# First norm of a two-layer encoder trunk: squares and means moved to other engines, inputs fetched in another order, and large tiles placed at multiples of 512 bytes

## The chip, the cores and the metric

The kernel runs on one core of one Trainium2 chip. The metric is the device time of one execution in microseconds (us); lower is better. A core has a tensor engine (TensorE, PE in the profile, with its weight loads as PEld), a vector engine (VectorE, DVE), a scalar engine (ScalarE, ACT), GpSimd (POOL) and a sync engine (SyncE, SP), which issues most of the transfers between the chip's memory and the on-chip SBUF. Each engine works through its own list of instructions in order and waits for the others by semaphores.

## What is computed

Two layers of a streaming encoder, on 512 tokens of 1,024 channels in float32. The change is in the first normalisation of the first layer; the rest of the program uses its result.

```python
def rms_norm(x, g):
    xf = x.astype(jnp.float32)
    y = xf * lax.rsqrt(jnp.mean(xf * xf, axis=-1, keepdims=True) + EPS_RMS)
    return (y * g.astype(jnp.float32)).astype(x.dtype)
...
    c_act = jax.nn.silu(c)
    for l in range(DEPTH):
        mod = c_act @ ada_w[l] + ada_b[l]
        sh1, sc1, gt1, sh2, sc2, gt2 = [m[:, None, :] for m in jnp.split(mod, 6, axis=-1)]
        h = rms_norm(x, norm1_g[l]) * (1 + sc1) + sh1
        p = h @ w_in[0]
        ...
        x = x + gt1 * (mixed @ w_out[l])
        h2 = rms_norm(x, norm2_g[l]) * (1 + sc2) + sh2
        gate, up = jnp.split(h2 @ w_gu[l], 2, axis=-1)
        x = x + gt2 * ((jax.nn.silu(gate) * up) @ w_down[l])
    return rms_norm(x, final_g)
```

## The kernel before, in words

**Layout.** Activations lie with channels on the 128 partitions and the 512 tokens along the row: x is eight tiles of 128 x 512, one for each block k of 128 channels (`xin`, named `xi` in the profile). A weight matrix comes in tiles of 128 x 1,024, eight blocks of 128 x 128.

**Products.** Nearly every product is made from three passes with float32r operands: weights and activations are each split into a high part (a rounded copy made by ScalarE) and a low part (the difference, made by VectorE or by an accumulating transfer that POOL issues), and `block` (L227) multiplies high by high, high by low and low by high. `hh` and `hl` are the parts of the normed activations, `whi` and `wlo` those of the weights, `f` (also `fh10` and such) those of the hidden layer in the feed-forward part. The feed-forward part uses 256-column passes (a seven-product scheme, `seven`), the rest mostly 512-column ones. A product of plain float32 operands (`nh` by `wr`, or the sums of the norm) takes two passes.

**Memory.** SBUF is filled by pools in the order in which they are opened: `const` (constants, L132), then `wraw`, `whl` (the split weights, L134), `hp` (`hh` and `hl`, L135) from the left, others such as `third`, `fp` (feed-forward weights and hidden parts) and `sm` from the right. No size is rounded up, so that each pool begins where the one before ends: in the built program the large tiles of `hp`, `whl` and `wraw` begin 96 bytes past a multiple of 512, those of `fp`, `dn`, `ya` and `third` 480 bytes past one, those of `w0`, `mx`, `wo` and `wk` 160 bytes past one.

**The head** (`head`, L294) comes before the two layers. SyncE issues, in this order: c copied to all 128 partitions (`cact`, 512 KB), the eight tiles of x (256 KB each), the first constants (`cst`) and the columns of biases (`cols`), two rows of `ada` (512 KB each), the first 384 columns of six tiles of `w_in` (`wr`), four more rows of `ada`, the other columns of `w_in`, and so on. ScalarE puts c through Silu (L310), then squares x tile by tile (`square`, L398 and L401), and VectorE adds the squares into one tile, `ssum` (L402). `rstd` (L404) then has TensorE sum `ssum` over the partitions against a column of 1/1024 (L410), ScalarE take the root (L413), VectorE the reciprocal (L414) and four 128 x 128 diagonals of it (`dg`, L417), and TensorE spread the result over all partitions by a product with ones (L422).

**After the norm** each channel block k needs `modulation` (L258: one row of `ada` times c, summed along the row; VectorE, an instruction of line 264), once for the scale and once for the shift, then VectorE's product of x and the norm (`nt`, L354), ScalarE's scale and shift (`nh`, L356), and the split into `hh` and `hl`. For k below `WHOLE` = 3 TensorE multiplies `nh` itself, in float32, by six tiles of `w_in`; from k = 3 on it uses the split parts.

**The order** of instructions on each engine is fixed when the program is built, by a scheduler that follows the code's order where `pinned` (for TensorE) or `exact` (for the other engines) is set.

Of the kernel before, what the change touches and what calls it, by code (L numbers as in the profile page):

```python
# [12 lines left out]
F32 = mybir.dt.float32  # L13
F32R = mybir.dt.float32r
AF = mybir.ActivationFunctionType
ALU = mybir.AluOpType
PSUM = bass.MemoryType.PSUM
DRAM = bass.MemoryType.DRAM

P = 128  # L20
D = 1024
S = 512
L = 2
KC = D // P
# [50 lines left out]

WHOLE = 3

EARLY = ((2, 5, 5, 4), (3, 6, 6, 6))
# [15 lines left out]
ALL = slice(0, S)  # L94
# [27 lines left out]
class Trunk:  # L122
    def __init__(self, ctx, tc, a, out):
# [6 lines left out]
        nc = self.nc  # L130
# [14 lines left out]
        self.omm = [self.const.tile([P, 15], F32, name=f"omm{l}") for l in range(L)]  # L145
        self.omka = [self.const.tile([P, 4], F32, name=f"omka{l}") for l in range(L)]
        self.xs = [self.dram.tile([P, S], F32, name=f"xs{k}") for k in range(KC)]
        self.yb = {
# [5 lines left out]
    def pool(self, **k):  # L154
        if "space" in k:
            return self.tc.tile_pool(**k)
        return self.tc.tile_pool(reuse_waits="tile", **k)
# [136 lines left out]
    def head(self, w0):  # L294
# [3 lines left out]
        self.cact = self.const.tile([P, D], F32, name="cact")  # L298
        nc.sync.dma_start(self.cact, a["c"].partition_broadcast(P))
        xin = [w0.tile([P, S], F32, name=f"xi{k}", bufs=1) for k in range(KC)]  # L300
        for k in range(KC):
            nc.sync.dma_start(xin[k], a["x"][k])
        at = CST["block"][0]
        nc.sync.dma_start(self.cst[:, 0:at], a["cst"][:, 0:at])
        nc.sync.dma_start(self.cols, a["cols"])
        nc.gpsimd.memset(self.ones, 1.0)
        nc.gpsimd.memset(self.mean, 1.0 / D)
        nc.gpsimd.memset(self.eps[:, 0:1], EPS_RMS)
        nc.gpsimd.memset(self.eps[:, 1:2], EPS_GN)
        nc.scalar.activation(self.cact, self.cact, AF.Silu)  # L310
        raws, ws = {}, []

        def rows(k):
            for i in (KC + k, k):
                raws[i] = self.rows(0, i, w0)

        raw = [w0.tile([P, D], F32, name=f"wr{i}", bufs=1) for i in range(KRV0)]
        cut = WHOLE * P
        rows(0)
        for i in range(KRV0):  # L320
# [4 lines left out]
        for i in range(KRV0):  # L325
            at = 0 if i == GV else cut
            nc.sync.dma_start(raw[i][:, at:], a["w_in"][0, i][:, at:])
        for k in range(KC):
            self.square(xin[k], k, ALL)
        self.soon(AF.Sqrt)  # L330
        self.new_h()
        rb = self.rstd(ALL)
        self.soon(AF.Sigmoid)
# [14 lines left out]
        for k in range(KC):  # L348
            if k >= WHOLE:
                rows(k)  # L350
            self.modulation(0, (KC + k, k), raws)
            self.gains(0, 0, k, k + 1)
# [50 lines left out]

    def rstd(self, hs, between=lambda: None):  # L404

        nc = self.nc
        n = (hs.stop - hs.start) // P
        st = self.m()
        for w in range(n):
            at = hs.start + w * P  # L410
            self.mm(st[:, w : w + 1], self.ssum[:, at : at + P], self.mean, start=True, stop=True)
        r = self.tmp.tile([P, 4], F32, tag="r4", name="r4", bufs=2)
        nc.scalar.activation(r[:, 0:n], st[:, 0:n], AF.Sqrt, bias=self.eps[:, 0:1])  # L413
        nc.vector.reciprocal(r[:, 0:n], r[:, 0:n])  # L414
        dg = self.tmp.tile([P, S], F32, tag="sq", name="dg", bufs=2)
        for w in range(n):
            nc.vector.tensor_scalar(  # L417
                dg[:, w * P : (w + 1) * P], self.c("ident"), r[:, w : w + 1], None, ALU.mult
            )
        between()  # L420
        rb = st[:, 0 : n * P]
        self.mm(rb, self.ones, dg[:, 0 : n * P], start=True, stop=True)  # L422
        return rb

    def turned(self, hs, g):
# [3 lines left out]
        st = self.m()  # L429
        r = self.tmp.tile([P, 4], F32, tag="r4", name="r4", bufs=2)  # L430
        out = self.hb[1].tile([P, n, D], F32, tag="hf1", name="y", bufs=1)
# [1235 lines left out]
```

## Time and profile before

| what | value |
|---|---|
| three runs | 1474.26, 1478.91 and 1479.97 us (median 1478.91) |
| profiled execution, its own time | 1479.65 us |
| span of its instructions | 1477.9 us |
| TensorE busy | 1429.7 us, 97% of the span |
| VectorE busy | 1087.3 us, 74% |
| ScalarE busy | 751.0 us, 51% |
| GpSimd busy | 246.8 us, 17% |
| mean rate of the transfers | 203 GB/s |

The profiled execution is one execution; its span runs from the first to the last instruction, and its own time is 1.75 us longer. A busy TensorE means that some pass was in it, not that it ran at its best pace: passes overlap, so the distance between the starts of two passes says more than the duration of one. "The granted clock" is the share of full speed (2.4 GHz) that TensorE was given. A row of the timeline gives the start in us, the duration in us, engine, line, operation, output<-inputs, shape and count, and in brackets how long the engine had been idle before it and what it waited for.

### The profile page before, as it was taken

The page shows a single profiled execution, that of the slowest core. Times are in us where ns is not written, and L with a number is a line of the kernel's source. Part 1 is how long each engine was busy: PE and PEld are TensorE (multiplying, and loading weights), DVE is VectorE, ACT ScalarE, POOL GpSimd, SP SyncE. Part 2 cuts the span into 40 slices and gives each one's busy share as a digit, 9 for nine tenths or more (in the row PEclk, how much of TensorE's full clock was granted, in tenths as well). Part 3 has the DMA queues.
Part 4 walks back from the last instruction along what each step waited for, and adds up shares of the span by engine and source line. Part 5 has one row for each costly group of instructions (what it writes and reads, how often), then busy time and mean ns, then how long its engine had stood idle before and what let it go on. Part 6 is the DMA issues. An engine that isn't in the chain of part 4 may idle for free. (4 is left out here: it accounts for less than half of the span.)

```text
span 1477.9 us, 25375 instructions
## 1 busy us (share of the span) xinstructions
PE 1429.7 (97%) x9982; PEld 1219.6 (83%) x9982; DVE 1087.3 (74%) x1846; ACT 751.0 (51%) x1031; POOL 246.8 (17%) x291
## 2 busy tenths in 40 slices
PE   5999998999999999999999999999999999999998
PEld 2767676777899999988897777877789999998887
DVE  7888958576788888876767685768578888887333
ACT  5576544344456656642336766443444656656221
POOL 0133321110022211100012334111102222110000
PEclk9999999999999999999999999999999999999999
DMA  8788689589839999778726747976974899885232
GB/s 319 235 268 238 193 227 254 148 261 271 236 101 230 234 215 226 179 251 287 260 87 180 181 113 168 261 176 191 289 235 131 208 219 223 192 187 169 87 100 71
DMA packets 112918, 299.28 MB, mean 203 GB/s; under 512 B 12128, under 2 KB 22624, under 8 KB 112800
## 3 DMA queue, kind: packets, MB, share of 16 engines
q1 hardware_dynamic: 90160, 227.93, 47.3%
q0 software_dynamic: 21776, 68.69, 25.5%
q8 instruction: 78, 1.28, 0.4%
q10 hardware_dynamic: 864, 1.05, 0.2%
q14 instruction: 40, 0.33, 0.1%
HBM read 269.84 MB, written 27.79 MB: 201 GB/s over the span
## 5 line engine op out<-in xcount | busy, mean ns | idle before, releaser
L221 PE MATMUL acc<-hh,whi 128*128 128x512 f32 (+1 forms) x1119 | 392.5, 357 | 0.2
L221 PE MATMUL acc<-hh,wlo 128*128 128x512 f32 (+1 forms) x1111 | 379.2, 346 | 8.3 <-DMA wlo<-in_w_in 7.5
L221 PE MATMUL acc<-hl,whi 128*128 128x512 f32 (+2 forms) x1119 | 369.3, 346 | 0.1
L195 ACT CAST whi<-raw 128x1024 fp32r<-128x1024 f32 x143 | 149.8, 1049 | 266.8 <-PE acc L221 175.2
L221 PEld LDWEIGHTS acc<-hh,wlo 128*128 128x128 f32 x1111 | 210.7, 190 | 36.7 <-DMA wlo<-in_w_in 9.2
L221 PEld LDWEIGHTS acc<-hh,whi 128*128 128x128 f32 x1119 | 212.1, 190 | 31.9 <-issue 2.4
L221 PEld LDWEIGHTS acc<-hl,whi 128*128 128x128 f32 (+1 forms) x1119 | 203.8, 189 | 26.4 <-issue 2.2
L201 DVE TENSOR_TENSOR wlo<-raw,whi 128x1024 fp32r<-128x1024 f32 x78 | 94.7, 1221 | 77.3 <-ACT whi L195 72.9
L221 PE MATMUL acc<-f,whi 128*128 128x512 f32 (+1 forms) x304 | 92.2, 386 | 0.0
L221 PE MATMUL m<-tl,f13h 128*128 128x256 f32 x304 | 86.0, 283 | 0.0
L221 PE MATMUL m<-th,f13l 128*128 128x256 f32 x304 | 86.0, 283 | 0.0
L221 PE MATMUL m<-th,f13h 128*128 128x256 f32 x304 | 85.9, 283 | 0.0
L241 ACT CAST f24h<-x 128x1024 fp32r<-128x1024 f32 x38 | 39.9, 1050 | 60.4 <-DVE x L241 60.4
L198 ACT ACTIVATE wlo<-raw 128x1024 fp32r<-128x1024 f32 x65 | 68.5, 1053 | 0.1
L221 PEld LDWEIGHTS acc<-f,whi 128*128 128x128 f32 x304 | 56.2, 188 | 12.3
L199 POOL DMA_DIRECT2D wlo<-in_w_in x41 | 35.9, 876 | 159.3 <-ACT wlo L198 159.3
L1283 POOL DMA_DIRECT2D f22l<-in_w_gu x38 | 32.8, 863 | 171.6 <-ACT f22l L241 164.4
L221 PE MATMUL acc<-f,wlo 128*128 128x512 f32 (+1 forms) x152 | 58.7, 386 | 0.0
L241 DVE TENSOR_TENSOR f24l<-x,f24h 128x1024 fp32r<-128x1024 f32 x38 | 46.5, 1224 | 16.3 <-ACT f24h L241 16.3
L221 PEld LDWEIGHTS m<-th,f13h 128*128 128x128 f32 x304 | 58.4, 192 | 0.0
L221 PEld LDWEIGHTS m<-th,f13l 128*128 128x128 f32 x304 | 58.4, 192 | 0.0
L221 PEld LDWEIGHTS m<-tl,f13h 128*128 128x128 f32 x304 | 58.2, 192 | 0.0
(338 smaller groups left out, 3434.0 us busy)
## 6 DMA issues: line engine op xcount, KB each, us to landing
raw<-in_w_in SPq DMA_DIRECT2D x63, 512.0 KB, 4.7
raw<-in_w_gu SPq DMA_DIRECT2D x50, 512.0 KB, 4.5
raw<-in_w_down SPq DMA_DIRECT2D x44, 512.0 KB, 3.5
wlo<-in_w_in POOLq DMA_DIRECT2D x41, 512.0 KB, 7.7
wlo<-in_w_gu POOLq DMA_DIRECT2D x40, 512.0 KB, 6.8
x<-in_w_gu SPq DMA_DIRECT2D x76, 256.0 KB, 4.4
row<-in_ada SPq DMA_DIRECT2D x30, 512.0 KB, 5.2
raw<-in_ada SPq DMA_DIRECT2D x25, 512.0 KB, 4.9
```

The lines of the kernel that those rows point to most:

```text
L195: self.on(nc.scalar, "copy")(hi, raw)
L198: nc.scalar.activation(lo, raw, AF.Copy, scale=-1.0)
L199: nc.gpsimd.dma_start(lo, src, accum_op=ALU.add)
L201: self.on(nc.vector, "tensor_tensor")(lo, raw, hi.bitcast(F32), ALU.subtract)
L221: i = (tensor.transpose if transpose else tensor.matmul)(*args, **k).ins
L241: return (lambda *a, **k: self.tc.keep_in_program_order(op(*a, **k))) if self.exact else op
L1283: nc.gpsimd.dma_start(lo, two[:, b], accum_op=ALU.add)
```

## The change

Four things change in the head, and one in the placing of tiles.

1. **Order of the transfers.** x goes ahead of c; c is fetched once, into one partition (4 KB), and TensorE spreads it over the partitions by a product with ones, in two halves (`spread`), from which ScalarE makes Silu. `cst`, `cols` and the first row of `ada` move in among the tiles of x.
2. **Squares.** VectorE squares six tiles of x, ScalarE two (k = 3 and 5). Nothing is added on VectorE; TensorE sums each square over the partitions as it comes and accumulates the eight in PSUM (32 products of one column, in place of 4).
3. **TensorE kept at work.** 16 products of ones by ones of 128 columns stand at its start, and five more on either side of the product that spreads the norm. Their results are not used.
4. **Order.** `modulation` for the first scale and the first shift is put ahead of and behind the norm's chain; two of the four diagonals go to ScalarE.
5. **Places.** A pad of 88 floats in `const` and one of 120 floats at the right edge move all pools: in the built program the tiles of `hp`, `whl`, `wraw`, `third`, `fp`, `dn`, `ya`, `w0`, `mx`, `wo` and `wk` begin at multiples of 512 bytes. Of the 7,538 float32r products 68 (in `sm` and `sl`) are left whose operands don't.

```diff
+PADS = (88, 120)
+WARM = (16, 5)
+ORDER = (0, 1, 2, 4, 3, 6, 5, 7)
...
+        self.const.tile([P, PADS[0]], F32, name="pad")
+        pool(name="edge", bufs=1, side="right").tile([P, PADS[1]], F32, name="edge")
...
-        nc.sync.dma_start(self.cact, a["c"].partition_broadcast(P))
         xin = [w0.tile([P, S], F32, name=f"xi{k}", bufs=1) for k in range(KC)]
+        c = w0.tile([1, D], F32, name="c", bufs=1)
+        raws, ws = {}, []
+
+        def rows(k, which=(KC, 0)):
+            for i in which:
+                raws[i + k] = self.rows(0, i + k, w0)
+
+        at = CST["block"][0]
         for k in range(KC):
             nc.sync.dma_start(xin[k], a["x"][k])
-        at = CST["block"][0]
-        nc.sync.dma_start(self.cst[:, 0:at], a["cst"][:, 0:at])
-        nc.sync.dma_start(self.cols, a["cols"])
+            if k == 1:
+                nc.sync.dma_start(c, a["c"].rearrange("(p n) -> p n", p=1))
+            if k == 3:
+                nc.sync.dma_start(self.cst[:, 0:at], a["cst"][:, 0:at])
+                nc.sync.dma_start(self.cols, a["cols"])
+            if k == 5:
+                rows(0, (KC,))
+        rows(0, (0,))
...
-        nc.scalar.activation(self.cact, self.cact, AF.Silu)
-        raws, ws = {}, []
-
-        def rows(k):
-            for i in (KC + k, k):
-                raws[i] = self.rows(0, i, w0)
+        self.soon(AF.Silu)
+        self.pinned = True
+        ps = [self.m() for _ in range(3)]
+        idle = lambda n: [self.mm(ps[2][:, 0:P], self.ones, self.ones, start=True, stop=True) for _ in range(n)]
+        idle(WARM[0])
+
+        def spread(i):
+            cs = slice(i * S, i * S + S)
+            self.mm(ps[i], self.ones[0:1, :], c[:, cs], start=True, stop=True)
+            nc.scalar.activation(self.cact[:, cs], ps[i], AF.Silu)
...
-        rows(0)
...
-        for k in range(KC):
-            self.square(xin[k], k, ALL)
-        self.soon(AF.Sqrt)
+        st = self.m()
+        for n, k in enumerate(ORDER):
+            if n in (1, 2):
+                spread(n - 1)
+                if n == 2:
+                    self.soon(AF.Sqrt)
+            sq = w0.tile([P, S], F32, tag="sq", name="sq", bufs=4)
+            if k in (3, 5):
+                nc.scalar.activation(sq, xin[k], AF.Square)
+            else:
+                nc.vector.tensor_tensor(sq, xin[k], xin[k], ALU.mult)
+            for w in range(4):
+                self.mm(
+                    st[:, w : w + 1], sq[:, w * P : w * P + P], self.mean, start=n == w == 0, stop=n == KC - 1 and w == 3
+                )
+        self.exact = True
+        self.modulation(0, (KC,), raws)
         self.new_h()
-        rb = self.rstd(ALL)
+        rb = self.rstd(ALL, lambda: idle(WARM[1]), st)
+        idle(WARM[1])
+        self.modulation(0, (0,), raws)
+        self.exact = self.pinned = False
...
-            self.modulation(0, (KC + k, k), raws)
+            if k:
+                self.modulation(0, (KC + k, k), raws)
...
-        for w in range(n):
-            nc.vector.tensor_scalar(
-                dg[:, w * P : (w + 1) * P], self.c("ident"), r[:, w : w + 1], None, ALU.mult
-            )
+        for w in range(n):
+            o = dg[:, w * P : (w + 1) * P]
+            if n == 4 and w % 2:
+                self.on(nc.scalar, "activation")(o, self.c("ident"), AF.Copy, scale=r[:, w : w + 1])
+            else:
+                self.on(nc.vector, "tensor_scalar")(o, self.c("ident"), r[:, w : w + 1], None, ALU.mult)
```

In the built programs the order of every engine is the same from the first `nh` on. Three places differ. TensorE, from its first instruction to the first product with `w_in` (`m` and `acc` are PSUM tiles, `mean` the column of 1/1024), before:

```order
L1656 UNCONDITIONAL_BRANCH
L221 MATMUL m<-mean,ssum 128x1 x4
L221 MATMUL m<-dg,ones 128x512
L221 MATMUL acc<-nh,wr_147 128x512
L221 MATMUL acc<-nh,wr_148 128x512
```

TensorE at the same place, changed:

```order
L1700 UNCONDITIONAL_BRANCH
L229 MATMUL m<-ones 128x128 x16
L229 MATMUL m<-mean,sq 128x1 x4
L229 MATMUL m<-c,ones 128x512
L229 MATMUL m<-mean,sq 128x1 x4
L229 MATMUL m<-c,ones 128x512
L229 MATMUL m<-mean,sq 128x1 x24
L229 MATMUL m<-ones 128x128 x5
L229 MATMUL m<-dg,ones 128x512
L229 MATMUL m<-ones 128x128 x5
L229 MATMUL acc<-nh,wr_177 128x512
L229 MATMUL acc<-nh,wr_178 128x512
```

Ahead of the norm's spreading there now stand 55 products in place of 4. ScalarE from its start to the norm's root (`r`), before:

```order
L310 ACT_TABLE_LOAD
L310 ACTIVATE cact<-cact 128x1024
L398 ACTIVATE ssum<-xi_124 128x512
L401 ACTIVATE sq<-xi_125 128x512
L401 ACTIVATE sq<-xi_126 128x512
L401 ACTIVATE sq<-xi_127 128x512
L401 ACTIVATE sq<-xi_128 128x512
L401 ACTIVATE sq<-xi_129 128x512
L401 ACTIVATE sq<-xi_130 128x512
L401 ACTIVATE sq<-xi_131 128x512
L391 ACT_TABLE_LOAD
L391 ACTIVATE soon<-eps 128x2
```

ScalarE at the same place, changed (`soon` is an activation that only calls for a function's table):

```order
L432 ACT_TABLE_LOAD
L432 ACTIVATE soon<-eps 128x2
L339 ACTIVATE cact<-m 128x512 x2
L432 ACT_TABLE_LOAD
L432 ACTIVATE soon<-eps 128x2
L359 ACTIVATE sq<-xi_131 128x512
L359 ACTIVATE sq<-xi_133 128x512
L455 ACTIVATE r_277<-m,eps 128x4
L249 ACTIVATE dg<-cst,r_277 128x128 x2
```

Two squares are left, and they stand behind both halves of Silu and the load of the root's table. SyncE's queue up to the first tile of `w_in`, changed (before: c, the eight tiles of x, `cst`, `cols`, two rows of `ada`):

```order
L317 DMA xi_128<-in_x 128x512
L317 DMA xi_129<-in_x 128x512
L319 DMA c<-in_c 1x1024
L317 DMA xi_130<-in_x 128x512
L317 DMA xi_131<-in_x 128x512
L321 DMA cst<-in_cst 128x128
L322 DMA cols<-in_cols 128x238
L317 DMA xi_132<-in_x 128x512
L317 DMA xi_133<-in_x 128x512
L263 DMA raw<-in_ada 128x1024
L317 DMA xi_134<-in_x 128x512
L317 DMA xi_135<-in_x 128x512
```

c no longer stands ahead of x; `cst`, `cols` and one row of `ada` now stand ahead of its last tile.

## Rows read from the trace of the kernel before

**Rows 1.** The page's first part: busy time, share of the span and instructions

```profile
PE 1429.7 (97%) x9982; PEld 1219.6 (83%) x9982; DVE 1087.3 (74%) x1846; ACT 751.0 (51%) x1031; POOL 246.8 (17%) x291
```

**Rows 2.** The timeline of the head, 0 to 28 us

```profile
0.74 0.21 POOL L306 MEMSET ones<- 128x128 f32 x1 [0.29 <-POOLq L1661]
...
5.43 1.06 ACT L310 ACTIVATE cact<-cact 128x1024 f32<-128x1024 f32 x1 [3.40 <-DMA cact<-in_c]
...
7.55 5.47 DVE L402 TENSOR_TENSOR ssum<-ssum,sq 128x512 f32<-128x512 f32 x7 [7.55 <-ACT sq L401]
...
12.12 1.28 ACT L391 ACT_TABLE_LOAD   x1
...
13.17 1.84 PE L221 MATMUL m<-mean,ssum 128*128 128x1 f32 x8 [13.17 <-POOL omka L383]
...
15.05 0.27 ACT L413 ACTIVATE r<-m,eps 128x4 f32<-128x4 f32 x1 [1.43 <-PE m L221]
...
15.56 0.88 DVE L417 TENSOR_SCALAR dg<-cst,r 128x128 f32<-128x128 f32 x4
16.35 1.28 DVE L264 CUSTOM_DVE_ANT_0 raw<-raw,cact,cols 128x1024 f32<-128x1024 f32 x1
...
16.58 2.04 PE L221 MATMUL m<-dg,ones 128*128 128x512 f32 x2 [1.57 <-DVE dg L417]
...
18.66 1.28 DVE L354 TENSOR_TENSOR nt<-xi,m 128x512 f32<-128x512 f32 x2 [1.03 <-PE m L221]
...
20.25 4.60 PE L221 MATMUL acc<-nh,wr 128*128 128x512 f32 x6 [1.63 <-ACT nh L356]
...
24.69 2.74 PE L221 MATMUL m<-nh,wr 128*128 128x512 f32 x6
```

**Rows 3.** The tiles of x (view of one tile): their issues, and issue to landing

```profile
L302 SPq DMA_DIRECT2D xi<-in_x x8: 328/432/652, 1.2 to 5.4; - x8
...
DMA to landing us min/median/max: 4.8/5.4/6.0
```

**Rows 4.** Busy time by stretch: length, PE, PEld, DVE, ACT, POOL, granted clock, DMA share, GB/s

```profile
10.00:20.00 10.00, 3.88 (x10) 2.28 (x10) 7.50 (x16) 5.62 (x9) 1.65 (x4) 1.00 1.05 396
...
20.00:38.74 18.74, 18.49 (x42) 8.37 (x43) 17.72 (x31) 9.30 (x15) 0.15 (x2) 1.00 0.77 298
...
160.37:167.19 6.82, 4.54 (x8) 2.29 (x9) 6.75 (x9) 2.13 (x3) 3.06 (x3) 0.50 0.18 71
```

**Rows 5.** The timeline where channel block k = 3 comes to TensorE

```profile
37.20 0.82 ACT L356 ACTIVATE nh<-nt,mods,gsc 128x512 f32<-128x512 f32 x1 [4.44 <-DVE mods L264]
...
38.74 1.10 PE L221 MATMUL acc<-hh,whi 128*128 128x512 f32 x4
```

**Rows 6.** The timeline at a later norm: weight loads of the one-column sums

```profile
398.22 0.52 PEld L221 LDWEIGHTS m<-mean,ssum 128*128 128x128 f32 x4 [1.41 <-DVE ssum L402]
```

**Rows 7.** The timeline of TensorE in the last w_down: 512-column passes, hh, then f

```profile
1419.64 0.39 PE L221 MATMUL acc<-hl,whi 128*128 128x512 f32 x1
...
1421.22 0.39 PE L221 MATMUL acc<-hh,wlo 128*128 128x512 f32 x1
...
1421.91 0.40 PE L221 MATMUL acc<-f,wlo 128*128 128x512 f32 x1
...
1423.31 0.40 PE L221 MATMUL acc<-f,wlo 128*128 128x512 f32 x1
```

**Rows 8.** The chain that ended last, in order of time: 256-column passes (start, us, what)

```profile
1176.25 2.88 PE m L221 x24
...
1182.01 1.42 PE m L221 x12
```

**Rows 9.** The timeline of TensorE: 256-column passes with weights from wk

```profile
413.79 0.63 PE L221 MATMUL acc<-hl,whi 128*128 128x256 f32 x4
...
415.20 0.64 PE L221 MATMUL acc<-hl,whi 128*128 128x256 f32 x4
```

**Rows 10.** Who waited for whom: us in total, times, longest

```profile
PE acc L221 <- DMA wlo<-in_w_in: 7.5, 4, 3.1
```

More of the change, by code (lines that the diff above doesn't have):

```diff
@@ L402, in square, with rstd @@
             nc.vector.tensor_tensor(self.ssum[:, hs], self.ssum[:, hs], sq[:, hs], ALU.add)
-    def rstd(self, hs, between=lambda: None):
+    def rstd(self, hs, between=lambda: None, st=None):
         nc = self.nc
         n = (hs.stop - hs.start) // P
-        st = self.m()
-        for w in range(n):
-            at = hs.start + w * P
-            self.mm(st[:, w : w + 1], self.ssum[:, at : at + P], self.mean, start=True, stop=True)
-        r = self.tmp.tile([P, 4], F32, tag="r4", name="r4", bufs=2)
+        if st is None:
+            st = self.m()
+            for w in range(n):
+                at = hs.start + w * P
+                self.mm(st[:, w : w + 1], self.ssum[:, at : at + P], self.mean, start=True, stop=True)
+        r = self.const.tile([P, 4], F32, tag="r4", name="r4", bufs=2)
         nc.scalar.activation(r[:, 0:n], st[:, 0:n], AF.Sqrt, bias=self.eps[:, 0:1])
-        nc.vector.reciprocal(r[:, 0:n], r[:, 0:n])
+        self.on(nc.vector, "reciprocal")(r[:, 0:n], r[:, 0:n])
         dg = self.tmp.tile([P, S], F32, tag="sq", name="dg", bufs=2)
         for w in range(n):
-            nc.vector.tensor_scalar(
-                dg[:, w * P : (w + 1) * P], self.c("ident"), r[:, w : w + 1], None, ALU.mult
-            )
+            o = dg[:, w * P : (w + 1) * P]
[3 more added lines that the diff above has]
+                self.on(nc.vector, "tensor_scalar")(o, self.c("ident"), r[:, w : w + 1], None, ALU.mult)
         between()
@@ L429, in turned @@
         st = self.m()
-        r = self.tmp.tile([P, 4], F32, tag="r4", name="r4", bufs=2)
+        r = self.const.tile([P, 4], F32, tag="r4", name="r4", bufs=2)
         out = self.hb[1].tile([P, n, D], F32, tag="hf1", name="y", bufs=1)
```

## The prediction

> **What bounds the kernel now.** I read the page's busy times first: TensorE is busy for 97% of the span [rows 1], so a change pays only where it takes time from TensorE's list or from what TensorE waits for. Next the timeline of the head [rows 2]: TensorE's first pass starts at 13.17 and its first product with a weight at 20.25, so the head is the longest stretch in which it has nothing to do. The chain there is plain to follow: squares and their sum end on VectorE at 13.02 (7.55 + 5.47), the eight passes of the means take 1.84, ScalarE's root starts at 15.05, the diagonals on VectorE at 15.56, their product with ones runs from 16.58 to 18.62, and VectorE's first `nt` starts at 18.66. TensorE is at half pace here: six passes with `nh` take 4.60 at 20.25 and the next six take 2.74.
>
> Then I looked at what holds TensorE after its start, since a shorter head is worth only what the next bound lets through. Between 20 and 38.74 VectorE is busy for 17.72 of 18.74 us [rows 4], and at k = 3 the supply is just in time: `nh` waits 4.44 us for VectorE, starts at 37.20, its rounded copy follows, and TensorE's first pass with it is at 38.74 [rows 5]. So from there on the clock that counts is VectorE's, counted from `nt` at 18.66; what TensorE gains between 20.25 and 38.74 by itself it would lose again waiting at k = 3. As no engine's order changes behind the first `nh`, the worth of all edits to the head is how much earlier that first `nt` starts.
>
> Last, the pace of the passes themselves, for the new places of the tiles. In the last part of `w_down` passes of one form and one weight pool stand side by side: with `hh` as the moving operand (96 past a multiple of 512, as the weights are) starts lie (1421.22 - 1419.64) / 7 = 0.226 apart, with `f` (480 past one) (1423.31 - 1421.91) / 6 = 0.233 [rows 7]. The only difference that I see between them is where the operands start.
>
> **The head, step by step.** *Transfers.* Before, the last tile of x is issued at 5.4 and lands 5.4 later, at about 10.8 [rows 3]. The change takes 512 KB (c) from ahead of it and puts 64 + 119 + 512 KB (`cst`, `cols`, a row of `ada`) there: 183 KB more, 0.5 us at 396 GB/s [rows 4]. I put it at 11.3. *Squares.* VectorE's square of a 128 x 512 tile costs about what an `nt` costs, 0.64 [rows 2], less than the spacing of the tiles; so they could be done at 12.0, against 13.02.
>
> *TensorE.* It is here that the time goes. The 16 idle products are 32 passes. A pass of this kind at half pace costs 1.84 / 8 = 0.23, and at full pace four weight loads take 0.52 together, the last one's tail included [rows 2, 6]; I take 0.11. In the trace it took from 20.25 to about 24.7 to come to full pace, and I let it need some 4 us from 1.0, when `ones` is set (0.74 + 0.21) [rows 2]. That is 17 passes at half pace and 15 at full, and the idle work ends near 6.6. Then the sums: 64 passes x 0.11 = 7.0, and the two products that spread c, four passes of 512 columns at 2.74 / 6 = 0.46, are 1.8. ScalarE's two squares stand behind the second half of Silu (0.6, half of 1.06 with its fixed part) and a table load of 1.28 [rows 2], and the fifth tile in TensorE's order needs the first of them: I count 1.0 of waiting. Sum: 6.6 + 7.0 + 1.8 + 1.0 = 16.4 for the root, against 15.05. TensorE, not the arrival of x, sets the end of the norm.
>
> *From the root to `nt`.* Before 3.61 (15.05 to 18.66). With two of four diagonals on ScalarE VectorE saves 2 x 0.22; the product with ones at full pace saves 1.0 of 2.04. But the row of `ada` (1.28 and the reading of its sum, some 1.36, as at 16.35 [rows 2]) still stands between the diagonals and `nt` on VectorE: 0.51 + 0.44 + 1.36 = 2.3. `nt` starts at 18.7, as before. The head's worth is **0.0**, between these bounds: -3.3 if the root follows the last tile at once (12.0 + 8 x 0.11 + 0.1 = 13.0, so `nt` at 15.4), and +11 if TensorE stays at half pace (first rival). The two products of five idle passes fit into waits of TensorE (1.1 us each) and cost nothing while it runs at full pace; 512 KB fewer to fetch is 0.2% of the traffic, and nothing waits for it.
>
> **The places of the tiles.** The built program has 684 passes with `f` against weights at 96, 634 with `hh` against weights at 480 or 160, and 1,608 with both at the same offset. If only the offset between the operands counts, all become equal, and 512-column passes go at 0.226: 684 x 0.007 = 4.8 saved in `w_down`, where nothing but TensorE sets the pace; and at the same price 4.4 for the 634. Of these last I count half, 2.2, since TensorE also waits there for others (7.5 us for low parts of `w_in` alone [rows 10]). For 256-column passes the sign turns round: 24 with equal offsets take 2.88, 0.120 each, 12 of the 1,088 at 96 against 480 take 1.42, 0.118 [rows 8], and 12 of the 384 at 96 against 160 take 1.41, 0.1175 [rows 9]. That gives back 1,088 x 0.0017 + 384 x 0.0025 = 2.8. Sum: -4.8 - 2.2 + 2.8 = -4.2; counting all of the 634 it is -6.4. I take **-4**. No row shows a tile at 0, and so both ends stay open: -16, if all passes run at the best pace seen (4,304 of 256 columns at 0.1175 instead of 0.119 on average: 7; and 9 for the others), and +11, if 0 is like the slow pairs (1,608 x 0.007).
>
> A rule speaks against this term. The Trainium skill says that TensorE reads its moving operand and its weights through two ports of their own, so that loading the next weights takes nothing from the pass that runs (TensorE: Matmul & The Clock Gate, Step-by-step: what each phase is for); by it the term would be 0. The trace doesn't agree: 0.226 and 0.233 for the same form of pass [rows 7].
>
> **Sum.** 1479.65 (the profiled execution's own time) + 0.0 - 4 = 1475.65. The median of the runs shown lies 0.74 below that execution; so I predict **1475.0**. A measurement of this kernel can tell 0.5%, 7.4 us, from no change.
>
> **The rivals.** (1) *Slower: the one-column sums don't bring TensorE to full pace, or let it fall back.* The idle work then ends at 1.0 + 32 x 0.23 = 8.4, the sums take 64 x 0.22 = 14.1, c's spreading 3.6: the root is at 26, 11 us later than before, and VectorE's stream with it: 1479.65 + 11 - 4 = 1486.7. It decides against the change once the root comes 4 us late, at 19. For it: such passes ran at half pace at 13.17 [rows 2], and at 160.37 the granted clock was 0.50 after a wait, with 4.54 of 6.82 us busy [rows 4]. Against it: idle products of 128 columns stand ahead of them. The Trainium skill says that half rate is the default and activity lifts it (TensorE: Matmul & The Clock Gate, Part 1: The HAM clock gate); what one-column passes count for isn't said there.
>
> (2) *The head gains in full*: sums that keep up with the arrival of x give -3.3, and the places in full -6.4: 1470.0. For it: 64 passes at 0.11 take no longer than the tiles need to arrive (4.8 to 6.0 after issues at 1.2 to 5.4 [rows 3]); against it: the idle products and c's spreading stand in the same list.
>
> (3) *The places give more*, all passes at the best pace seen: 1479.65 - 16 = 1463.7.
>
> (4) *The change doesn't do what it says*: neither the head nor the places move anything, as the skill's rule on the ports has it: 1479.6. For it: VectorE's bound at k = 3.
>
> **How the numbers follow.** Forecast 0.47, rival (1) 0.10, (2) 0.18, (3) 0.08, (4) 0.17. The range of 1464 to 1486 takes in the forecast, (2), (4), most of (3) and the low part of (1), where half pace holds for a part of the sums only. Faster by over 0.5% are (2) and (3) and a little of the forecast: 0.29. Slower are (1) and a tail of unfavourable places: 0.11. Within 0.5%: 0.60. The likeliest case alone spans 1471 to 1479.
>
> **What would show it.** Right: the root near 16.4 and `nt` near 18.7; TensorE without a gap from 1.0 on, its sums 0.11 apart; a new wait of about 2 us at k = 3; passes of `f` in `w_down` 0.226 apart and those of 256 columns all at 0.120. Wrong: a root before 14 or after 19; passes of `f` still at 0.233, or 512-column passes well below 0.226; VectorE's stream from `nt` to k = 3 shorter than the 18.5 us of before; a granted clock of 0.50 in other stretches than before.

## The result and the profile after

The changed kernel takes 1485.34 us (median of 14 runs, 1481.97 to 1493.17) against 1478.32 for the kernel before, measured on the same chip beside it: a ratio of 1.0061, 95% interval 1.0046 to 1.0076. The ratio leaves out one run of the kernel before that took 4585.17 us, and the quotient of the two medians is 1.0047. The forecast was 1475.0, a little faster; the change is slower by 0.6%. The profiled execution took 1482.6, with a span of 1480.5.

The page's first part says that TensorE is busier than before [rows 1], by 18.6 us and 112 passes, which are 56 products of two passes each (26 idle ones, 28 more sums and two that spread c):

```profile
PE 1448.3 (98%) x10094; PEld 1244.0 (84%) x10094; DVE 1084.9 (73%) x1843; ACT 747.6 (51%) x1029; POOL 245.6 (17%) x291
```

The timeline of the head of the changed kernel (start, length, engine, line, what; in brackets the idle time before it and what ended that) stands against [rows 2]:

```profile
1.00 6.79 PE L229 MATMUL m<-ones 128*128 128x128 f32 x32 [1.00 <-POOL mean L327]
...
7.62 0.95 PE L229 MATMUL m<-mean,sq 128*128 128x1 f32 x8
...
8.50 1.12 PE L229 MATMUL m<-c,ones 1*128 1x512 f32 x2
...
9.55 1.05 PE L229 MATMUL m<-mean,sq 128*128 128x1 f32 x8
...
10.54 2.02 PE L229 MATMUL m<-c,ones 1*128 1x512 f32 x2
11.50 0.69 DVE L361 TENSOR_TENSOR sq<-xi 128x512 f32<-128x512 f32 x1 [2.50 <-DMA xi<-in_x]
...
12.49 10.40 PE L229 MATMUL m<-mean,sq 128*128 128x1 f32 x48
...
16.10 0.69 DVE L361 TENSOR_TENSOR sq<-xi 128x512 f32<-128x512 f32 x1 [3.91 <-PE m L229]
...
22.93 0.26 ACT L455 ACTIVATE r<-m,eps 128x4 f32<-128x4 f32 x1 [7.18 <-PE m L229]
...
25.02 1.91 PE L229 MATMUL m<-dg,ones 128*128 128x512 f32 x2
...
26.98 1.28 DVE L395 TENSOR_TENSOR nt<-xi,m 128x512 f32<-128x512 f32 x2 [1.85 <-PE m L229]
```

Read it by TensorE. Eight one-column passes take 0.95 at 7.62 and eight 1.05 at 9.55; then two passes that spread c take 2.02 where two took 1.12 before, and 48 one-column passes take 10.40, 0.217 each. ScalarE's root starts at 22.93 instead of 15.05, and the first `nt` at 26.98 instead of 18.66: 8.3 us later. The squares are not what is late. The last one waits 3.91 us for TensorE (for a buffer that the sums had not yet read), and ScalarE waits 7.18 for the sums.

The same stretches in the view of busy time by stretch (length, then PE, PEld, DVE, ACT and POOL busy, granted clock, DMA share, GB/s) show what halved the pace. The edges are those at which the granted clock changes:

```profile
1.00:7.21 6.21, 6.21 (x29) 6.21 (x30) 2.05 (x3) 1.23 (x2) 0.05 (x2) 1.00 0.80 235
7.21:10.62 3.41, 3.41 (x24) 2.62 (x23) 0.69 (x1) 0.60 (x1) 0.73 (x4) 1.00 0.99 368
10.62:27.69 17.07, 17.07 (x67) 14.53 (x68) 5.20 (x12) 5.57 (x10) 0.00 (x0) 0.50 0.62 226
27.69:36.00 8.31, 8.21 (x25) 3.96 (x25) 7.66 (x15) 3.49 (x5) 0.00 (x0) 1.00 1.00 349
```

The first record of the clock is at 7.21; the 1.00 in the row ahead of it is no measurement. (In the trace of the kernel before the first record is at 23.84, so the 1.00 of [rows 4] for 10 to 20 isn't one either; the eight one-column passes there went at half pace.) From 7.21 to 10.62 the granted clock is at its full level (2.4 GHz), then for 17.07 us at half (1.2 GHz), although TensorE is never idle in that stretch; it is full again from 27.69.

The second part of the change did to the passes what was forecast. In the last `w_down` of the changed kernel, the stretch of [rows 7]:

```profile
1423.31 0.39 PE L229 MATMUL acc<-hh,wlo 128*128 128x512 f32 x1
...
1424.67 0.39 PE L229 MATMUL acc<-hh,wlo 128*128 128x512 f32 x1
...
1425.35 0.39 PE L229 MATMUL acc<-f,wlo 128*128 128x512 f32 x1
...
1427.39 0.39 PE L229 MATMUL acc<-f,wlo 128*128 128x512 f32 x1
```

With `hh` (1424.67 - 1423.31) / 6 = 0.227, with `f` (1427.39 - 1425.35) / 9 = 0.227, where it was 0.233. Yet a wait has grown elsewhere. Around the first product with `w_out`'s weights in the second layer, the timeline of TensorE in the kernel before:

```profile
1076.76 0.50 PE L221 MATMUL acc<-mh,whi 128*128 128x512 f32 x1 [0.43 <-ACT mh L245]
1077.49 0.51 PE L221 MATMUL acc<-ml,whi 128*128 128x512 f32 x1 [0.23 <-DVE ml L246]
...
1079.23 0.51 PE L221 MATMUL acc<-mh,wlo 128*128 128x512 f32 x1 [0.53 <-DMA wlo<-in_w_out]
```

and in the changed kernel:

```profile
1079.21 0.51 PE L229 MATMUL acc<-mh,whi 128*128 128x512 f32 x1 [0.85 <-ACT mh L253]
1079.93 0.51 PE L229 MATMUL acc<-ml,whi 128*128 128x512 f32 x1 [0.22 <-DVE ml L254]
...
1082.72 0.80 PE L229 MATMUL acc<-mh,wlo 128*128 128x512 f32 x1 [1.58 <-DMA wlo<-in_w_out]
```

In these two executions the waits have grown from 1.19 to 2.65 us, and the pass at 1082.72 lasts 0.80: the granted clock was at half from 1082.40 to 1085.82, which it was not there before.

### The profile page after: what moved, and what is told of

Its sections match the earlier page's. It is cut to its first block, busy times and chain, and to the rows that moved or that the text cites. A ratio compares the mean times of both kernels' runs of the same rounds, so it can differ in the third digit from the quotient of the medians.

```text
span 1480.5 us, 25589 instructions
## 1 busy us (share of the span) xinstructions
PE 1448.3 (98%) x10094; PEld 1244.0 (84%) x10094; DVE 1084.9 (73%) x1843; ACT 747.6 (51%) x1029; POOL 245.6 (17%) x291
## 3 DMA queue, kind: packets, MB, share of 16 engines
q10 hardware_dynamic: 864, 1.05, 0.2%
```

## The experiments

All but run 7, which measures a pace, were compared with runs of the kernel before on the same chip; ratios are to those, with 95% intervals.

**1. The places alone.** The filler tiles and `r4` in the constants, with the old head:

```diff
+PADS = (88, 120)
+        self.const.tile([P, PADS[0]], F32, name="pad")
+        pool(name="edge", bufs=1, side="right").tile([P, PADS[1]], F32, name="edge")
-        r = self.tmp.tile([P, 4], F32, tag="r4", name="r4", bufs=2)
+        r = self.const.tile([P, 4], F32, tag="r4", name="r4", bufs=2)
```

> The kernel before with the two filler tiles (88 and 120 columns) and the small tile r4 in the constants, so that the large tiles begin where they do in the change; its head is the old one. Theory (the change loses about 8 us in the head and wins about 5 by the places): about 5 us under before, 1473 to 1474 in a median of 1478, the 512-column passes of w_down at 0.227 apart instead of 0.233 and the 256-column passes at 0.120. Rival A (the places do nothing or cost something, the whole difference is in the head): 1478 or more. Rival B (the places give the 16 us of the open end): about 1463.

Measured: 1476.94 against 1478.04, ratio 0.9994 (0.9980 to 1.0008). The passes are as expected. At the full clock, and with waits left out, the starts of some 2,900 passes of 512 columns stand 227.6 ns apart on average, where before they stood 230.2 apart, and those of some 4,200 passes of 256 columns 119.9, where before it was 119.2. That is 7.7 us saved and 3.0 given back, or 4.7 in all. The time is not as expected: about 1 us under before, not 5. The timeline of TensorE at the place named above shows one reason:

```profile
1070.26 0.50 PE L224 MATMUL acc<-mh,whi 128*128 128x512 f32 x1 [1.24 <-ACT mh L248]
1070.98 0.50 PE L224 MATMUL acc<-ml,whi 128*128 128x512 f32 x1 [0.22 <-DVE ml L249]
...
1074.00 0.80 PE L224 MATMUL acc<-mh,wlo 128*128 128x512 f32 x1 [1.85 <-DMA wlo<-in_w_out]
```

Waits of 3.3 us against 1.2 before. The stretches of the same kernel:

```profile
1070.00:1073.37 3.37, 1.68 (x5) 0.86 (x5) 1.77 (x2) 1.35 (x3) 0.00 (x0) 1.00 0.88 239
1073.37:1080.19 6.82, 6.19 (x15) 4.85 (x16) 5.26 (x9) 0.63 (x1) 0.00 (x0) 0.50 0.66 207
```

TensorE was busy for half of 3.37 us, and then had the half clock for 6.82.

**2. The head alone.** The change without the two filler tiles and with `r4` among the temporaries; the reverse of the diff above.

> The changed kernel without the filler tiles and with r4 among the temporaries again: the new head, the old places. Theory: root at about 22.9 and nt at about 27 as in the change, so about 8 us above before plus nothing else: 1486 to 1491. Rival A (places nothing): the time of the change, about 1485. Rival B: about 1494 to 1500.

Measured: 1485.84, ratio 1.0048 (1.0031 to 1.0066). That is the change's own time within the noise: the head is the whole loss, and beside it the places again show next to nothing. The time is just under what was expected, and the traced head is earlier than expected, with the root at 20.48 instead of 22.9 and `nt` at 24.53 instead of 27:

```profile
10.66 2.30 PE L227 MATMUL m<-mean,sq 128*128 128x1 f32 x16
...
13.45 6.99 PE L227 MATMUL m<-mean,sq 128*128 128x1 f32 x32 [0.49 <-ACT sq L357]
...
20.48 0.26 ACT L453 ACTIVATE r<-m,eps 128x4 f32<-128x4 f32 x1 [6.56 <-PE m L227]
```

Here the granted clock fell to half at 12.09 and stayed there to 25.74. Nearly half of the 64 one-column passes ran at the full pace, not a quarter as in the change. So how long the full clock lasts into these sums differs from one execution to the next; that it falls before they end is seen in both.

**3. The sums with as many products, but 128 columns wide.** The edit changes no other count, order or transfer:

```diff
+        wide = w0.tile([P, P], F32, name="wide", bufs=1)
+        nc.gpsimd.memset(wide, 1.0 / D)
-                    st[:, w : w + 1], sq[:, w * P : w * P + P], self.mean, start=n == w == 0, stop=n == KC - 1 and w == 3
+                    st[:, w * P : w * P + P], sq[:, w * P : w * P + P], wide, start=n == w == 0, stop=n == KC - 1 and w == 3
+        made = st is not None
+        means = st.rearrange("p (w n) -> p w n", n=P)[:, :, 0] if made else st[:, 0:n]
-        nc.scalar.activation(r[:, 0:n], st[:, 0:n], AF.Sqrt, bias=self.eps[:, 0:1])
+        nc.scalar.activation(r[:, 0:n], means, AF.Sqrt, bias=self.eps[:, 0:1])
```

> The change with one edit: each square is summed against a 128-column tile of 1/D instead of a column, so the 32 products give 128 equal columns each and the root reads every 128th; as many products, passes and weight loads as in the change, each with 128 columns instead of one. Theory (the granted clock falls to its half level because the one-column products leave TensorE with nearly nothing to do): the clock stays at its full level through the sums, the passes stand 0.11 apart instead of 0.21, root at 14.5 to 16.5, nt at 17.5 to 19.5, and the time 1473 to 1476. Rival (the number of products before the root is what counts, or the order in which x arrives): root at 22 to 24 again, and the time that of the change, about 1485, or later.

Measured: 1476.6, ratio 1.0000 (0.9985 to 1.0015), 8.7 us under the change. Its head:

```profile
1.00 6.07 PE L229 MATMUL m<-ones 128*128 128x128 f32 x32 [1.00 <-POOL ones L326]
...
11.09 5.62 PE L229 MATMUL m<-wide,sq 128*128 128x128 f32 x48
...
16.75 0.26 ACT L459 ACTIVATE r<-m,eps 128x4 f32<-128x4 f32 x1 [2.92 <-PE m L229]
...
18.00 1.12 PE L229 MATMUL m<-dg,ones 128*128 128x512 f32 x2 [0.18 <-ACT dg L249]
...
19.17 1.28 DVE L397 TENSOR_TENSOR nt<-xi,m 128x512 f32<-128x512 f32 x2 [0.22 <-PE m L229]
```

48 passes of 128 columns take 5.62 where 48 of one column took 10.40. The granted clock is full from its first record at 5.71 to 159.3. This decides the question of the head: with the same number of passes and loads, the width alone moves the root by 6.2 us and `nt` by 7.8. The root came 0.25 later than the latest value expected, the time 0.6.

**4. No idle products**, `WARM = (0, 0)` in the change, which has 26 of them (16 ahead of the sums, twice five behind; the expectation says 42).

> The change without its 42 idle products (16 ahead of the sums, twice 5 behind). Theory: in the change the granted clock falls to its half level at 10.6 although the idle products had brought it up at 7.2, so they buy the first 8 one-column passes and nothing else: without them the clock is at its half level throughout, the 64 passes stand 0.213 apart and end where they ended, root at 21 to 24, nt at 25 to 28, the time within 3 us of the change (1483 to 1489). Rival (the idle products take time that the sums need): root 3 us earlier or more, the time 1482 or less.

Measured, as expected: 1485.9, ratio 1.0067 (1.0042 to 1.0093). The head:

```profile
4.33 1.84 PE L229 MATMUL m<-mean,sq 128*128 128x1 f32 x8 [4.33 <-DVE sq L361]
...
11.89 10.40 PE L229 MATMUL m<-mean,sq 128*128 128x1 f32 x48
...
22.32 0.26 ACT L455 ACTIVATE r<-m,eps 128x4 f32<-128x4 f32 x1 [7.18 <-PE m L229]
...
25.69 1.29 DVE L395 TENSOR_TENSOR nt<-xi,m 128x512 f32<-128x512 f32 x2 [1.17 <-PE m L229]
```

The 48 passes take the same 10.40, and the root is 0.6 us earlier than in the change. The idle work that was to keep TensorE at work bought no time in front of one-column sums: it takes 6.8 us itself, and some of the passes behind it are faster. With wide sums (run 3) the clock stays up behind it. Whether wide sums would keep it up without idle work was not tried.

**5. Four sums instead of 32.** The change's early x, spread of c, idle products (16, 2, 12, 5) and split diagonals, but squares on ScalarE and their running sum on VectorE as before:

```diff
-        for n, k in enumerate(ORDER):
...
+        for k in range(KC):
+            if k in (3, 4):
+                spread(k - 3)
+                idle(WARM[k - 2])
+            self.square(xin[k], k, ALL)
```

> The change's places, its early x, its spread of c by TensorE, its idle products (16, 2, 12 and 5 of them) and its split diagonal, but the squares on ScalarE and their running sum on VectorE as in before, so that TensorE sums four products only. Theory (with 32 products gone from the way to the root, the root follows the last arriving x): root at about 14 to 15, nt at 16.5 to 18 where the clock stays up and 18 to 19 where it falls during the wait, and the time 1470 to 1475. Rival (ScalarE's eight squares and the two Silu halves, one engine, now end last): root at 17 or later, the time 1476 or more.

Measured: 1478.97, ratio 1.0010 (0.9996 to 1.0024): the head as expected, the time not. The root is at 13.99 and `nt` at 16.41:

```profile
12.93 1.02 PE L229 MATMUL m<-mean,ssum 128*128 128x1 f32 x8 [0.74 <-DVE ssum L431]
...
13.99 0.26 ACT L443 ACTIVATE r<-m,eps 128x4 f32<-128x4 f32 x1 [0.62 <-PE m L229]
...
16.41 1.28 DVE L383 TENSOR_TENSOR nt<-xi,m 128x512 f32<-128x512 f32 x2 [0.22 <-PE m L229]
```

So this earlier head is not worth its lead. The next table, worked out from the profiled traces, follows the same passes through the runs: when each starts, against its start in the kernel before (us, minus is earlier). The list of TensorE's passes from the first `nh` on is the same in all of them.

```
in before at   pass             places   four sums   wide sums   the change
   20.25       acc<-nh,wr       -0.46     -2.25       +0.50       +8.31
   38.04       acc<-hl,whi      +0.57     -4.03       -1.27       +6.55
   40.14       acc<-hh,wlo      +0.56     -2.42       -0.18       +8.14
  209.61       m<-cst,v         +0.98     -0.67       -1.14       +9.59
  269.81       m<-vt,ar         -4.42     -5.02       -2.76       +4.38
  510.45       m<-tl,f13h       -3.99     -4.10       -3.44       +4.73
  630.92       acc<-f,whi       -3.44     -3.56       -2.90       +5.27
  751.03       m<-f,wr          -5.41     -5.53       -4.87       +3.30
 1053.41       acc<-yah,whi     -6.82     -6.04       -5.91       +2.78
 1083.48       acc<-mh,wlo      -2.39     -4.42       -3.60       +4.91
 1444.39       acc<-fh,whi      -4.32     -4.47       -5.56       +2.94
```

The lead of "four sums" over "places" is 4.6 us at 38, 3.0 at 40 (k = 3, where TensorE waits for VectorE's stream), 1.6 at 210, 0.6 at 270 and 0.1 at 510. The lag of the change against "places" is 8.8 at the start and still 7.3 at the end. In these traces a late head costs nearly all of its delay, and an early one gains nothing. The step of 4 to 5 between 210 and 270 in three of the columns is one wait for a low part of `w_in` that the profiled execution of before had at 222, with 3.4 us at half clock behind it:

```profile
225.66 0.79 PE L221 MATMUL acc<-hh,wlo 128*128 128x512 f32 x1 [3.13 <-DMA wlo<-in_w_in]
```

With the old places run 10 has this wait too and run 11 doesn't; with those of the change runs 13 and 14 have it and run 12 doesn't. So it is no effect of the places. Where the lead of "four sums" goes is not settled by one trace each: over its 12 runs that kernel also lost more to the half clock than run 1 did, 12.4 us on average against 10.0 (the loss is worked out as under "What the places are worth").

**6. All large tiles at 96 past a multiple of 512**, `PADS = (112, 96)` in run 1.

> The kernel before with filler tiles of 112 and 96 columns, so that all large tiles begin 96 bytes past a multiple of 512, weights and moving tiles alike. Theory (what counts is that weights and moving tile begin at the same offset in 512 bytes, not that it is zero): the passes as with the places of the change, 512 columns at 0.227 and 256 columns at 0.120, the f passes of w_down 0.226 to 0.228 apart, and the time within 2 us of the run with the places alone (1475 to 1479). Rival (a multiple of 512 is what counts): f passes at 0.232 to 0.234, the time 1478 or more.

Measured: 1477.99, ratio 1.0008 (0.9994 to 1.0023), within 1.1 us of run 1, with its passes of 512 columns 227.6 apart on average and those with `f` 0.227. So it is the distance between the two tiles that counts, and multiples of 512 are one way among others to make it zero.

**7. The pace by itself.** The kernel computes none of the reference: it is 256 pairs of places, 12 float32r passes each at either size.

> A kernel that computes none of the reference: 12 float32r passes each for all pairs of 16 places of the moving tile and 16 of the weights, 32 bytes apart in 512, with 256 and with 512 columns. Theory (the pace is set by the distance between the two places, not by either alone): equal places give 226 to 228 ns for 512 columns and 119 to 121 for 256, wherever they lie; with weights 64 bytes on, 512 columns take 230 to 234 and 256 columns 113 to 118. Rival (what matters is each tile's own place, a multiple of 512 or of 64): the pace goes with one of the two alone, and equal places differ among themselves by more than 3 ns.

Measured, from the distances of the starts at the full clock; each line is the mean over 15 places of the moving tile of the median pace of 12 passes (the first moving tile, whose passes waited for data, is left out):

```
weights ahead of moving tile, bytes, modulo 256    512 columns, ns    256 columns, ns
   0                                                  227.1              120.0
  32                                                  232.0              117.1
  64                                                  235.4              117.4 (113 to 118)
  96                                                  233.4              117.5
 128                                                  231.6              119.6
 160                                                  231.7              119.1
 192                                                  229.5              118.0
 224                                                  234.0              118.0
```

The values for a distance and for the distance plus 256 agree to 0.2. Equal places give 227 to 228 and 120 wherever they lie. So equal places are the best of these for 512 columns and the worst for 256, and the pace goes with the distance, not with either place alone. At 64 the 512-column passes are slower than the 230 to 234 expected. The Trainium skill says that TensorE reads its weights and its moving operand through two ports of their own, so that loading the next weights takes no read bandwidth from the running pass (TensorE: Matmul & The Clock Gate, Step-by-step: what each phase is for); by that alone all lines should be alike. For float32r passes of these sizes they are not, and the measurement decides; by what way the two come to touch stays open.

**8. One group of 256-column tiles moved off its weights' place.** Run 1 with 16 more columns behind the sums of h:

```diff
+            tp.tile([P, 16], F32, name="apart")
             tail, made = iter(()), None
```

> The places of the change with the old head, and 16 more columns among the sums of h (th and tl), which moves these moving tiles to 448 past a multiple of 512 while their weights f stay at 0: 1368 passes of 256 columns get weights that begin 64 bytes on. In before 374 such passes with that distance (96 and 160) stood 116.9 ns apart, and those with equal offsets 119.9. Theory (a pass of 256 columns is shorter where the two begin at different offsets): 117 instead of 120 in these, 4 us less, 1472 to 1474. Rival (that difference came from the stage, not from the places): 120 as before, the time that of the places alone, 1475 to 1479.

Measured: 1469.26, ratio 0.9948 (0.9932 to 0.9964), 7.7 us under run 1, twice what was expected, since the 1,368 passes go at 113.9 on average:

```profile
445.90 0.28 PE L224 MATMUL m<-th,f13h 128*128 128x256 f32 x1
...
446.58 0.28 PE L224 MATMUL m<-th,f13h 128*128 128x256 f32 x1
...
447.26 0.28 PE L224 MATMUL m<-th,f13h 128*128 128x256 f32 x1
```

That is 12 passes in 1.36, 0.113 each; 1,368 x 0.006 = 8.2. Run 7 has the same 113 in some pairs 64 bytes apart and 118 in most; why the passes settle at the one or the other stays open. In run 1 the same passes stand 0.120 apart.

**9. The low halves of `w_out`'s first two weights on VectorE**, in run 1, instead of by ScalarE and an accumulating DMA:

```diff
+                        was, self.by_dma = self.by_dma, False
                         outs.append(wout(len(outs)))
+                        self.by_dma = was
```

> The places of the change with the old head, and the low halves of the first two weights of w_out made by VectorE instead of by ScalarE and an accumulating DMA, in both layers. In the run with the places alone TensorE waited 1.8 for such a DMA at 1074 and then had the half clock from 1073.4 to 1080.2, and 4.4 us of what the places had saved were gone behind it. Theory (the places' gain is given back in that wait and the slow stretch behind it): the wait is gone, the clock stays at its full level there, and the time is 2 to 5 us under the run with the places alone: 1472 to 1475. Rival (something else is late right behind it, the products mh on ScalarE and VectorE): a wait of 1 us or more stays there, and the time is 1476 or more.

Measured: 1471.18, ratio 0.9966 (0.9951 to 0.9981), 5.8 us under run 1. The waits that are left at this place:

```profile
1067.57 0.49 PE L224 MATMUL acc<-mh,whi 128*128 128x512 f32 x1 [0.53 <-ACT mh L248]
1068.30 0.50 PE L224 MATMUL acc<-ml,whi 128*128 128x512 f32 x1 [0.23 <-DVE ml L249]
```

No half clock follows. That looked like the places' gain found again; runs 10 and 11 were made to check it.

**10 and 11. The same edit, and both edits, at the old places.**

> The kernel before, old head and old places, with the low halves of w_out's first two weights made by VectorE. With the places of the change this edit gave 1471.2 against 1476.9. Theory (the wait for these low halves appears because the shorter passes bring TensorE there sooner, and takes the places' gain back): at the old places the edit is worth 0 to 3 us, 1475 to 1478, so that without this wait the places are worth 4 to 7. Rival (the edit is a gain of its own): 1471 to 1473 here too, and the places are worth 0 to 2.

> The kernel before with both edits at the old places: low halves on VectorE, and 16 more columns among the sums of h, which puts th and tl at 416 and leaves their weights at 480. With the places of the change the two gave 1462.7. Theory: the 1368 passes go at 113 here too, and the old places cost 4 to 7 us against the new: 1467 to 1470. Rival: 1462 to 1465.

Measured: the low halves alone 1473.85, ratio 0.9970 (0.9952 to 0.9987), between the two expectations and nearer to the rival; so this edit is for the greater part a gain of its own. The wait for such a transfer that the kernel before has at 1079 is 0.53 us, far less than the 4 to 5 us gained; what else the edit saves was not isolated. Both edits 1468.46, ratio 0.9924 (0.9894 to 0.9953), as the theory had it.

**12 to 14. Both edits at the new places, under three heads**: the old one, the change's with wide sums, and that with four sums.

> The old head with the places of the change, the sums of h 64 bytes from their weights' place, and the low halves of w_out's first two weights on VectorE. Theory (the 1368 shorter passes lie in stages without a wait, the wait for w_out's low halves behind another stage; the two gains add): 7.7 us (run with t apart against the places alone) and 5.8 us (run with the low halves against the same) under the 1477 of the places alone: 1462 to 1466. Rival (what the shorter passes save is waited for at the next transfer): 1467 or more.

> The same two edits on the change with sums against 128 columns of 1/D. Theory (a head as early as the old one is worth what the old one is): within 2 us of the old head with the same edits, 1462 to 1467. Rival (the clock's early full level costs slow stretches later): 1468 or more.

> The same two edits on the head with squares on ScalarE and four one-column products, whose nh products began 2 us ahead of the old head's and whose lead was gone by 270 us. Theory (the transfers of the first layer set the time of that stage, whatever the head): the lead is gone again by 270 us and the time is within 2 us of the old head with the same edits, 1462 to 1467. Rival (the lead was lost at the wait that the low halves now avoid): 2 us or more under it, 1459 to 1462.

Measured: 1462.72, ratio 0.9899 (0.9878 to 0.9920); 1466.28, 0.9908 (0.9895 to 0.9921); 1465.03, 0.9912 (0.9896 to 0.9927). The two gains add, and the three heads can't be told apart: "four sums" is no faster here either. Its traced execution is no clean test of the expectation, though. The granted clock was at half from 15.90 to 19.32 in its head, so that its `nh` products began 0.6 us ahead of the old head's and not 2, and by 270 it had met the wait at 222 that the trace with the old head doesn't have. The version with the old head is 1% faster than the kernel before and 1.5% faster than the change.

**What the places are worth.** Four pairs differ in the places alone, three times the new places and once those of run 6 against the old. The part lost at half clock is worked out as span x (1 - mean granted clock), over the runs of each kernel; each figure is the difference new (or run 6) minus old places, after subtracting each kernel's difference to before on its own chip (us):

```
pair                       mean time   lost at half clock   the rest
old head, runs 1, before     -0.3           +2.9              -3.2
old head, runs 6, before     +0.7           +2.5              -1.8
with low halves, 9, 10       -1.1           +1.9              -3.0
with both edits, 12, 11      -3.5           +1.8              -5.4
```

The rest shows the shorter passes, 2 to 5 us of them, and about 2 us go to more time at half clock. By the spread of the runs none of the four differences in mean time is clear of zero. Behind the head a slow stretch was found to follow a wait at each place that was looked at: 160 in [rows 4], where TensorE was busy for 2.12 of the 3.41 us before, 225 in the kernel before, 1073 in run 1. That shorter passes make more of them, because TensorE reaches the same data sooner, fits these pairs but was not isolated.

## Why the prediction was wrong

**The step that failed** is *TensorE* in the head: "Then the sums: 64 passes x 0.11 = 7.0". It took for granted that the full pace, once reached, lasts through the sums. In the traced execution it lasted for the first 16 passes. The 48 others took 10.40 (0.217 each), with the granted clock at 0.50 from 10.62. So the root stood at 22.93 instead of 16.4, and the head cost 8.3 instead of 0.0. Run 3 shows the cause: with 128 columns in place of one the clock stays at full and the loss is gone.

The rest of that working comes out as soon as the clock holds, in part by luck. In run 3 the root is at 16.75 and `nt` at 19.17, against 16.4 and 18.7 forecast; the idle products end at 7.1 there, forecast 6.6. From 6.91 the sums and the spreading of c take 9.8, as much as forecast, but the 1.0 counted for waiting is not there, and the passes take that much more (0.117 each instead of 0.11, and 2.1 for c instead of 1.8). The stretch from the root to `nt` is 2.42 in run 3, forecast 2.3; at half clock in the change it is 4.05. VectorE's stream was right: in the change from `nt` at 26.98 to `nh` of k = 3 it is 18.52, before it was 18.54 [rows 2, 5]. The new wait at k = 3 is 1.36, forecast about 2:

```profile
45.50 0.81 ACT L397 ACTIVATE nh<-nt,mods,gsc 128x512 f32<-128x512 f32 x1 [4.44 <-DVE mods L272]
...
47.02 0.96 PE L229 MATMUL acc<-hh,whi 128*128 128x512 f32 x3 [1.36 <-ACT hh L253]
```

**Rival (1) is what happened**: root at 26 and 1486.7 were its numbers, 22.93 and 1485.34 came. Its root is 3 us too late because the full pace did come for a while: the idle work ended 0.8 earlier than it had it, the first 16 one-column passes took 1.9 instead of 3.5, and the spreading of c 3.0 instead of 3.6. That its time is so near is partly luck, since it also took 3 us more off for the places than they gave. It had 0.10. What spoke for it was in the rows: eight one-column passes at half pace at 13.17. Since TensorE had been idle ahead of them, they could not tell a clock that had not yet risen from one that such passes don't hold up. The one argument against it was that idle products of 128 columns stand ahead, and these turned out to be worth no time (run 4).

**The places**: the pace was forecast to 0.001 (0.227 for `f`, 0.120 for all of 256 columns), and in the stretches without waits the sum comes out near it. From 630.92 to 751.03, one layer's `w_down`, the run with the places alone gains 1.97 us in the table, where half of the 4.8 for `f` was 2.4 (of the 684 passes counted for it the trace has 588 with `f`, `fh` and `fl`); from 510.45 to 630.92 it loses 0.55 over passes of 256 columns, the sign forecast. As a term of the time, -4 was too much: -1.1 by the medians, interval -3.0 to +1.2. The step that failed there is that the 4.8 were counted in full because nothing but TensorE sets the pace in `w_down`: what a stage saves was not followed into the next ones. In that trace 2.40 us are gained from 269.81 to 1053.41 and 1.93 from 1083.48 to 1444.39, but 4.43 are lost between 1053.41 and 1083.48, behind a wait for a transfer and a stretch of half clock. The open end of -16 was not reached by the change; the pairs at distance 64 show that such a gain lies in the 256-column passes, at places other than the change's.

**The range** held the time, 1485.34 being just below its upper end, which the low part of rival (1) had set. The forecast itself had the wrong sign: 1475.0, a little faster.

## What to carry to other kernels

Where TensorE is to sum over partitions in many small products on the critical path, look at the granted clock of exactly that stretch: keep the products wide, or leave most of the sum to another engine and give TensorE a few. Here both took the loss away and neither beat the old head. Ask of each term whether the stage it lies in waits for data: a shorter head or shorter passes were worth nothing there, while a delay was paid nearly in full. For the pace, give weights and moving tiles equal places modulo 256 bytes for 512-column passes (in the time of this kernel that gain did not show), and try places 64 bytes apart where all passes with a tile have 256 columns.

## What the runs showed that was not expected

- The granted clock was at half for 17.07 us through which TensorE was busy without a gap; what it ran when the clock fell were one-column passes and two that spread a row. With 128-column passes in their place it stayed at full.
- 32 idle passes of 128 columns from 1.00 on were followed by the first record of the full clock at 7.21, 5.71 and 4.66 in the traces of three kernels (the change, runs 3 and 5).
- The pace of float32r passes depends on the distance of weights and moving tile modulo 256 bytes: 227 to 235 ns for 512 columns, 117 to 120 for 256, and a second settled pace of 113 for 256 columns at a distance of 64.
- Moving two low halves per layer from an accumulating DMA to VectorE saved 4 to 6 us, though VectorE is the second busiest engine; why so much was not isolated.
